# A retention state for the first 256 keys, and a new order for the start of layer 0, in a two-layer hybrid trunk

## The chip, the cores and the metric

The kernel runs on one core of one Trainium2 chip. The metric is the device time of one execution in microseconds (us). The engines are TensorE (PE; its weight loads are listed as PEld), VectorE (DVE), ScalarE (ACT), GpSimd (POOL) and SyncE (SP, whose queue issues most DMAs).

## The reference

Two layers work on 528 positions (16 meta tokens and 512 real ones) of width 1024, all in float32. Each layer: RMSNorm, one input projection, eight heads of forgetting attention (FoX) and four heads of retention, an output projection, then a SwiGLU FFN of width 2816. The last norm drops the meta tokens.

```python
def fox_attention(q, k, v, logf):
    c = cumsum(logf)                              # per head, over positions
    s = q_t.k_s / sqrt(64) + c[t] - c[s]          # s <= t, else -inf
    return softmax(s) @ v
def retention_chunkwise(q, k, v):
    # o_t = sum_{s<=t} gamma_h^(t-s) (q_t.k_s) v_s
    # computed by chunks: inside a chunk directly, older chunks by a state
    state = chunk_dec * state + (k * k_dec)^T v
    ...
def hybrid_layer(h, ...):
    xn = rmsnorm(h, attn_norm_g)
    fq, fk, fv, flog, rq, rk, rv, rg = split(xn @ w_in)
    logf = log_sigmoid(flog + b_fgate)
    fox_out = fox_attention(fq, fk, fv, logf)
    ret = head_groupnorm(retention(rotate(rq), rotate(rk) * 128**-0.5, rv))
    h = h + concat(fox_out, silu(rg) * ret) @ w_out
    hn = rmsnorm(h, ffn_norm_g)
    return h + (silu(hn @ w_gate) * (hn @ w_up)) @ w_down
```

## The kernel before, in words

Activations lie transposed: features on the 128 partitions, the 528 positions along the free axis; `h[0..7]` hold the residual. Every product is made of float32 operands that are split into a rounded high part (`fp32r`) and a low rest, so one product takes three matmuls (high x high, high x low, low x high). The high part is a ScalarE copy, the low part a VectorE subtraction (`split`, lines 150 and 151); for weights it is `convert` (lines 199 and 202, the latter on GpSimd where the job says `pool`).

A projection of 128 output columns is eight steps, one per 128 features, of six matmuls each: three pairs over the column halves of 264 (line 225), or three over 512 columns where only real positions count. Results go to `psd`, two double banks of PSUM; scores and smaller products use `psa`, four banks. The order of TensorE's work is written out by hand: `layer` makes a list of steps, and `merge` puts attention's and retention's steps between the projection's steps at given places. The other engines' order comes from a scheduler that takes instructions by program order and readiness; `tc.high_priority()` moves an instruction forward, and `pin` keeps those that it marks in program order.

**Start of layer 0.** The scaled `x` and the weights are built while the first DMAs land. TensorE then runs the first head pair's queries and keys step by step side by side (`qk`), the forget gates' product (line 389), the norm's column sums (line 298), and goes on with the values and with retention's first projections. The norm's factor `R` (`col_rstd`: Ln, Exp and one Newton step) comes late, so the query and key results wait in `psd` for `R`: `q_done` (line 442) and `k_done` (line 456) scale them straight out of PSUM. `forget_sums` (lines 403 to 412) makes the log-sigmoid of the gates, its running sum `z2`, and the split of it into `f_tiles`. `k_done` puts that, chosen per head by `pick`, into the key tile's other rows ("own rows", line 467). The first FoX scores (line 519) need them. The order was

```python
plan += [squares] + qk[:-2] + [first_parts] + gates + qk[-2:] + stats
        + [queries scaled] + sums + [keys scaled]
plan += v + [ropes]
```

**Retention of a head** (`ret_steps`): `values` transposes and centres the values; `scores` multiplies a key block of 128 by all queries at or after it (line 722), then by the decay table `dec` (line 727), and splits the result into `rsh` and `rsl`; `product` multiplies by the values (line 756). Key blocks start at 0, 128, 256, 384 and 512 (the last has 16 keys). Score steps take the blocks (0), (1) and (2, 3, 4); a block's width is 528, 400, 272, 144 and 16 queries (512 for block 0 in layer 1, which drops the meta queries). The result is copied out of PSUM to `d` by ScalarE (line 764). Ten steps per head are placed by `ret_places` (values, three scores, three products, weighing, norm, gate).

**End.** The last FFN product is made in two column parts, of 272 and 240 positions. For the second the squares of the eight `h` tiles are summed: tiles 0 to 4 on VectorE into `acc`, tiles 5, 6 and 7 separately, and TensorE adds the four parts with a matrix of ones in float32 (line 1164). The root, its Newton step and the output multiplies and DMAs follow.

Of the kernel before, what the change touches and what calls it, by code (L numbers as in the profile page):

```python
# [34 lines left out]
HALF = T // 2  # L35
PSTEP = 416
# [3 lines left out]
def hybrid_kernel(ctx, tc, x_t, w_in, w_fl, w_out, w_gate, w_up, w_down, vecs, b_fg, rope, decay, mask, ident, out_t):  # L40
# [14 lines left out]
    nc.vector.memset(msk[:, 0:T - 128], 0.0)  # L55
# [11 lines left out]
    nc.vector.memset(onec, 1.0)  # L67

# [136 lines left out]
    def dense_steps(src, parts, pool=False, banks=False, ahead=(1, 4), own=None, wait=None):  # L205

        j = len(jobs)
        jobs.append({"src": src, "pool": pool, "own": own})  # L210

        def chunk(k0, k, n, xs, cols, ps, done):
            def go():
                convert(j)
                if k == 0:
                    t = [psum_a() for _ in cols] if banks else psum()
                    ps.append(t)
                    ps.append(t if banks else [t[:, b] for b in range(2)])
                size = jobs[j]["w"][0][0]
                _, hi, lo = jobs[j]["w"][(k0 + k) // size]  # L220
                wk = (k0 + k) % size
                xh, xl = xs(k)
                for i, (w, x) in enumerate(((hi, xh), (hi, xl), (lo, xh))):
                    for b, (c0, c1) in enumerate(cols):
                        nc.tensor.matmul(ps[1][b][:, 0:c1 - c0], w[:, wk, :], x[:, c0:c1],  # L225
                                         start=(k == 0 and i == 0), stop=(k == n - 1 and i == 2))
                if k == n - 1:
                    done(ps[0]) if wait is None else wait.append(lambda: done(ps[0]))
# [62 lines left out]
    def col_rstd(parts, n, cols, rname):  # L291
# [63 lines left out]
    def rstd(st, cols, rname="R"):  # L355

        st["R"] = col_rstd(st["parts"], D, cols, rname)
# [41 lines left out]
    def forget_sums(l, st):  # L399
        z = st["z"]  # L400
        z2 = tt("z2")[0:FH]
        with ExitStack() if l else tc.high_priority():
            nc.vector.scalar_tensor_tensor(z, z, RSC, st["R"][0:FH, :], ALU.mult, ALU.mult)
            nc.scalar.activation(z2, z, AF.Abs, bias=bfg[:, l:l + 1])
            nc.scalar.activation(z2, z2, AF.Exp, scale=-1.0)
            nc.scalar.activation(z2, z2, AF.Ln, bias=onec[0:FH])
        nc.vector.tensor_scalar(z, z, bfg[:, l:l + 1], 0.0, ALU.add, ALU.min)
        nc.vector.tensor_sub(z, z2, z)
        nc.vector.tensor_tensor_scan(z2, z, z, 0.0, ALU.add, ALU.max)
        with ExitStack() if l else tc.high_priority():  # L410
            nc.scalar.copy(f_tiles[0][0:FH], z2)
            nc.vector.tensor_sub(f_tiles[0][32:32 + FH], z2, f_tiles[0][0:FH].bitcast(F32))
# [20 lines left out]
    def fox_dense(l, g, ly, real, st):  # L433
# [5 lines left out]
        def q_done(ps):  # L439
            tq = tt("tq")  # L440
            with tc.high_priority() if first else ExitStack():
                nc.vector.scalar_tensor_tensor(sv(tq, real), pv(ps, real), RSC / 8.0, sv(ly["R"], real), ALU.mult, ALU.mult)  # L442
# [11 lines left out]
        def k_done(ps):  # L454
            tk = tt("tq")
            nc.vector.scalar_tensor_tensor(sv(tk, False), pv(ps, False), RSC, sv(ly["R"], False), ALU.mult, ALU.mult)
            st["k"] = []
            for s in range(2):
# [8 lines left out]
                (nc.gpsimd if g else nc.vector).tensor_scalar(kc[b0:b0 + 32 + FH, :], f_tiles[0].bitcast(F32), pick[:, hd:hd + 1], 0.0, ALU.mult, ALU.add)  # L467
# [156 lines left out]
    def ret_dense(l, hd, ly, real, st, which):  # L624
        QC = REAL if real else FULL

        def rope_done(nm, rl):
            def go(ps):
# [4 lines left out]
                t1 = tt("tq")  # L633
# [5 lines left out]
                st[nm] = (th, tl)  # L639
            return go  # L640
# [7 lines left out]
        def g_done(ps):  # L648
# [10 lines left out]
            nc.vector.tensor_scalar_max(u, x, -80.0)  # L659
# [11 lines left out]
    def ret_steps(l, hd, st, real):  # L671
# [23 lines left out]
        def q_start(j):  # L695
            return max(qlo, KOFF[j] if j < 4 else SEQ)


        def scores(grp):
            if grp[0] == 0:  # L700
                dec = at("dec", F32, (128, T), 1)
                nc.sync.dma_start(dec, decay[hd])
                st["dec"] = dec
# [4 lines left out]
            ps = None  # L708
            reads = []
            for j in grp:  # L710
                q0 = q_start(j)
                d0 = q0 - KOFF[j]
                n = T - q0
                kn = KLEN[j]
                for c0, c1 in (((0, HALF), (HALF, n)) if n > 512 else ((0, n),)):
                    if ps is None or n > 512:
                        ps = psum_a()
                    off = used if len(grp) > 1 else 0
                    sc = ps[0:kn, off:off + c1 - c0]
                    ko = KOFF[j]  # L720
                    for i, (a, b) in enumerate(((kh, qh), (kh, ql), (kl, qh))):
                        nc.tensor.matmul(sc, a[:, ko:ko + kn], b[:, q0 + c0:q0 + c1], start=(i == 0), stop=(i == 2))  # L722
                    reads.append((kn, slice(used + c0, used + c1), sc, slice(d0 + c0, d0 + c1)))
                kept[j] = (used, grp[0])
                used += n
# [14 lines left out]

        def product(grp):
# [4 lines left out]
            po, d = st["po"], st["d"]  # L746
            for j in grp:
                used, g0 = kept[j]
                q0 = q_start(j)
                qa = max(q0, META)  # L750
                sh, sl = kept["t", g0]
                if j == 4:
                    nc.tensor.matmul(po[:, SEQ - META:SEQ], vh[:, 4, :], kept["e"], start=False, stop=True)
                else:
                    for i, (a, b) in enumerate(((vh, sh), (vh, sl), (vl, sh))):
                        nc.tensor.matmul(po[:, qa - META:SEQ], a[:, j, :], b[:, used + qa - q0:used + T - q0],  # L756
                                         start=(j == 0 and i == 0), stop=False)
                if j == 0 and not real:
# [3 lines left out]
                    nc.scalar.copy(d[:, 0:META], pm[:, 0:META])  # L762
                if j == 4:
                    nc.scalar.copy(d[:, META:T], po)
# [55 lines left out]
    def ffn(l, st, real, last):  # L820
# [269 lines left out]
        else:  # L1090
# [34 lines left out]
            def square_b(m):  # L1125
                if m == 0:
                    t = fft("S", F32, (128, 6, w), 2)
                    fin["one"] = [t[:, i, 0:nb] for i in range(3)]
                    fin["acc"], fin["rb"], fin["tb"] = (t[:, i, 0:nb] for i in range(3, 6))
                    d = fin["acc"]  # L1130
                elif m < NK - 3:
                    fin["sq", m] = d = tt("sq")[:, 0:nb]
                else:
                    d = fin["one"][m - NK + 3]
# [111 lines left out]
    def layer(l):  # L1246
# [59 lines left out]
        stats = [lambda: rstd(ly, FULL)]  # L1306
# [5 lines left out]

        sums = [lambda: forget_sums(l, ly)]
# [7 lines left out]
        def ret_places(hd, *places):  # L1321

            f = rs[hd]
            return list(zip(places, (f[0], f[1], f[2], f[4], f[3], f[5], f[6], f[7], f[8], f[9])))
# [29 lines left out]
def _tables():  # L1354
# [4 lines left out]
    decay = np.zeros((RH, 128, T), np.float64)  # L1359
    k = np.arange(128)[:, None]  # L1360
    q = np.arange(T)[None, :]
    for hd in range(RH):
        decay[hd] = np.where(q >= k, np.exp(np.maximum(q - k, 0) * math.log(GAMMA[hd])), 0.0)
    decay = (decay * 128.0 ** -0.5).astype(np.float32)
# [59 lines left out]
```

## Time and profile before

| | us |
|---|---|
| median of 3 runs | 1268.74 (1267.4 to 1270.0) |
| profiled execution, device time | 1268.53 |
| its span, first to last instruction | 1266.7 |

| engine | busy us | share of the span |
|---|---|---|
| PE | 1251.2 | 99% |
| PEld | 1194.1 | 94% |
| DVE | 991.9 | 78% |
| ACT | 704.8 | 56% |
| POOL | 273.3 | 22% |

Matmuls are pipelined: a matmul's listed duration is longer than the distance to the next one's start, and the distance is what counts. In the timeline a row has the start, the duration, the engine and line, the operation, output and inputs, and in brackets how long the engine idled before it and what ended that. "x2" means that two instructions were merged into the row. PEclk is the granted share of TensorE's full clock. A line of the profile can be that of a helper.

### The profile page before, as it was taken

How to read it: one execution, taken by the hardware profiler on the slowest of the kernel's cores; microseconds unless marked ns; L12 is line 12 of the kernel's file. 1: busy time of each engine (PE TensorE's matmuls, PEld its weight loads, DVE VectorE, ACT ScalarE, POOL GpSimd, SP SyncE). 2: the span in 40 equal slices, each digit the busy share in tenths (PEclk: the TensorE clock that was granted, in tenths of full speed). 3: DMA queues.
4: the chain of work that ended last, by engine and by line, in shares of the span. 5: the costliest groups of instructions: out<-in, count | busy, mean ns of one | idle time of the engine just before them, and what ended most of it. 6: DMA issues, size and time to landing. Idle time of an engine off the chain costs nothing.

```text
span 1266.7 us, 23526 instructions
## 1 busy us (share of the span) xinstructions
PE 1251.2 (99%) x9225; PEld 1194.1 (94%) x9225; DVE 991.9 (78%) x1804; ACT 704.8 (56%) x1301; POOL 273.3 (22%) x539
## 2 busy tenths in 40 slices
PE   9999999999999999999999999999999999999997
PEld 8899999999999999999999989998789999999996
DVE  8887756779988888887786877567899888888867
ACT  6766655676444444444466766557764444444445
POOL 3455546420000000000126556554100000000000
PEclk9999999999999999999999999999999999999999
DMA  6122222223333333332322122222223333333321
GB/s 218 50 76 75 76 77 72 72 67 118 104 97 100 100 101 100 101 101 84 101 77 84 60 86 74 70 90 67 100 94 123 100 101 101 100 101 101 100 84 67
DMA packets 43342, 116.19 MB, mean 92 GB/s; under 512 B 5088, under 2 KB 12000, under 8 KB 43232
## 3 DMA queue, kind: packets, MB, share of 16 engines
q1 hardware_dynamic: 42800, 114.41, 28.1%
q8 instruction: 72, 1.18, 0.4%
q14 instruction: 38, 0.31, 0.1%
q10 hardware_dynamic: 432, 0.29, 0.1%
HBM read 112.58 MB, written 2.10 MB: 91 GB/s over the span
## 4 chain that ended last, share of the span: by engine, by line
PE 93%; ACT 3%; DVE 3%; issue 1%; DMA 0%; ACTq 0%; DVEq 0%
PE psd L225 30%; PE psa L907 18%; PE psd L1042 14%; PE psd L907 13%; PE psa L225 5%; PE psa L1042 4%; PE psa L429 2%; PE psa L519 2%; PE psa L589 1%; PE psa L756 1%; PE psa L722 1%; ACT whi L199 1%; PE psa L298 0%; ACT xh L327 0%; DMA raw<-w_in 0%
## 5 line engine op out<-in xcount | busy, mean ns | idle before, releaser
L202 POOL TENSOR_TENSOR wlo<-raw,whi 128x128 fp32r<-128x128 f32 x504 | 258.2, 548 | 260.1 <-ACT whi L199 259.7
L225 PE MATMUL psd<-xh,whi 128*128 128x264 f32 (+1 forms) x792 | 195.5, 314 | 0.2 <-DVE tq L442 0.2
L225 PE MATMUL psd<-xl,whi 128*128 128x264 f32 (+1 forms) x792 | 186.7, 303 | 0.6 <-DVE xl L328 0.6
L225 PE MATMUL psd<-xh,wlo 128*128 128x264 f32 (+1 forms) x792 | 187.0, 304 | 0.0
L225 PEld LDWEIGHTS psd<-xh,whi 128*128 128x128 f32 x792 | 128.6, 189 | 5.0 <-issue 0.6
L225 PEld LDWEIGHTS psd<-xh,wlo 128*128 128x128 f32 x792 | 127.2, 188 | 6.2 <-DVE wlo L202 0.4
L225 PEld LDWEIGHTS psd<-xl,whi 128*128 128x128 f32 x792 | 127.8, 189 | 5.4 <-DVE xl L328 1.4
L199 ACT CAST whi<-raw 128x512 fp32r<-128x512 f32 (+1 forms) x168 | 97.9, 613 | 41.5 <-PE psd L225 28.4
L895 ACT CAST whi<-raw 128x1024 fp32r<-128x1024 f32 (+2 forms) x62 | 54.9, 885 | 51.3 <-PE psd L907 39.8
L895 ACT CAST fwhi<-raw 128x1024 fp32r<-128x1024 f32 (+2 forms) x62 | 55.6, 897 | 47.5 <-PE psd L907 40.0
L122 POOL MEMSET kc<- 64x528 f32 x2 | 1.1, 533 | 345.4 <-PE psa L907 345.4
L896 DVE TENSOR_TENSOR wlo<-raw,whi 128x1024 fp32r<-128x1024 f32 (+2 forms) x62 | 62.9, 1014 | 12.7 <-ACT whi L895 12.6
L896 DVE TENSOR_TENSOR fwlo<-raw,fwhi 128x1024 fp32r<-128x1024 f32 (+2 forms) x62 | 64.0, 1032 | 11.1 <-ACT fwhi L895 10.9
L907 PE MATMUL psa<-th,whi 128*128 128x264 f32 (+1 forms) x232 | 65.4, 282 | 0.0
L907 PE MATMUL psa<-th,wlo 128*128 128x264 f32 (+1 forms) x232 | 65.4, 282 | 0.0
L907 PE MATMUL psa<-tl,whi 128*128 128x264 f32 (+1 forms) x232 | 65.3, 282 | 0.0
L907 PE MATMUL psa<-th,fwhi 128*128 128x264 f32 (+1 forms) x224 | 63.4, 283 | 0.0
L907 PE MATMUL psa<-tl,fwhi 128*128 128x264 f32 (+1 forms) x224 | 63.3, 283 | 0.0
L907 PE MATMUL psa<-th,fwlo 128*128 128x264 f32 (+1 forms) x224 | 63.2, 282 | 0.0
L536 ACT ACTIVATE pr<-pr,nmax 128x144 f32<-128x144 f32 (+1 forms) x64 | 36.8, 576 | 45.4 <-DVE nmax L523 26.1
L895 ACT CAST fwhi<-S 128x1024 fp32r<-128x1024 f32 x20 | 21.0, 1049 | 68.6 <-PE psa L907 66.5
L973 ACT COPY e<-psa 128x264 f32<-128x264 f32 (+1 forms) x114 | 42.8, 376 | 28.4 <-PE psa L907 24.1
(365 smaller groups left out, 4041.2 us busy)
## 6 DMA issues: line engine op xcount, KB each, us to landing
raw<-w_in SPq DMA_DIRECT2D x54, 512.0 KB, 3.5
raw<-w_gate SPq DMA_DIRECT2D x44, 512.0 KB, 3.9
fraw<-w_up SPq DMA_DIRECT2D x38, 512.0 KB, 3.5
raw<-w_down SPq DMA_DIRECT2D x64, 256.0 KB, 2.9
raw<-w_out SPq DMA_DIRECT2D x16, 512.0 KB, 3.4
raw<-w_down SPq DMA_DIRECT2D x32, 192.0 KB, 2.5
raw<-w_up SPq DMA_DIRECT2D x6, 512.0 KB, 3.5
h<-x_t SPq DMA_DIRECT2D x8, 264.0 KB, 4.5
```

The lines of the kernel that those rows point to most:

```text
L199: pin(nc.scalar.copy(hi, job["raw"][:, c0:c1]), pinned)
L202: pin(sub(lo[:, c:c + step], job["raw"][:, c0 + c:c0 + c + step], hi[:, c:c + step].bitcast(F32)), pinned)
L225: nc.tensor.matmul(ps[1][b][:, 0:c1 - c0], w[:, wk, :], x[:, c0:c1], start=(k == 0 and i == 0), stop=(k == n - 1 and i == 2))
L429: nc.tensor.transpose(ps[:, 128 * j:128 * j + 128], src[:, o:o + 128], idt)
L519: nc.tensor.matmul(sc[0:nq, 0:c1 - c0], qq[:, q0:q0 + nq], kk[:, c0:c1], start=(i == 0), stop=(i == 1))
L536: nc.scalar.activation(pr, pr, AF.Exp, bias=nmax[0:nq], scale=-1.0, accum_out=rsum)
L589: nc.tensor.matmul(po[:, c0:SEQ], v[:, j, :], pp[:, j, META + c0:T], start=(j == 0 and i == 0), stop=(j == 4))
L895: nc.scalar.copy(hi, src)
L896: nc.vector.tensor_sub(lo, src, hi.bitcast(F32))
L907: nc.tensor.matmul(bank()[:, 0:b.shape[-1]], a[:, o + k, :], b, start=(fresh and k == 0 and i == 0), stop=(k == n - 1 and i == 2), skip_gr ...
L973: nc.scalar.copy(self.t["e"][:, i], self.t["x"][:, 0:w])
L1042: nc.tensor.matmul(v[:, 0:c1 - c0], a[:, s * n + k, :], b[:, c0:c1], start=(k == 0 and i == 0), stop=(k == n - 1 and i == 2))
```

## The change

Three groups of edits. **Retention:** keys 0 to 255 no longer meet the queries from 256 on directly. Their keys are transposed and weighted by decay (`keys`), multiplied with their values into a 128 x 128 state (`memory`), and the second `product` multiplies that state with the queries from 256 on. The score steps are (0, 1), now up to query 256 only, and (2, 3, 4), whose decay table no longer depends on the query; the query's decay is applied when the result leaves PSUM, on VectorE. The step list is again ten long: values, scores (0, 1), keys, memory, scores (2, 3, 4), product (0, 1), product (2, 3, 4), weigh, norm, gate, in the places of before. The table grows from 528 to 962 columns, and the float32 keys are kept in a tile of their own, `rkf`.

**Layer 0's start:** the first queries and keys are copied aside, unscaled, by ScalarE (`aside`); the next weights' cast is pinned behind the copies; the gates' chain comes before the scaling of queries and keys; one subtraction of the chain is folded into the scan; the chain's rest gets high priority; the norm's Ln and Exp are pinned; the second head's own rows go to ScalarE.

**Small orders:** the mask's memset goes to GpSimd; the gate's lower bound is made by another VectorE instruction; at the end tile 5's square is added on VectorE, and three parts go to TensorE instead of four.

```diff
+CUT = 256
+DOFF = (0, 0, CUT, T, 2 * T - CUT - 128)
+DEC = DOFF[4] + META + T - CUT + 2
...
-    nc.vector.memset(msk[:, 0:T - 128], 0.0)
...
+    nc.gpsimd.memset(msk[:, 0:T - 128], 0.0)
...
-                nc.scalar.activation(r[:, c0:c1], v, AF.Ln, bias=epsc, scale=1.0 / n)
-            nc.scalar.activation(r[:, c_all], r[:, c_all], AF.Exp, scale=-0.5)
+                pin(nc.scalar.activation(r[:, c0:c1], v, AF.Ln, bias=epsc, scale=1.0 / n), pinned)
+            pin(nc.scalar.activation(r[:, c_all], r[:, c_all], AF.Exp, scale=-0.5), pinned)
...
-        nc.vector.tensor_scalar(z, z, bfg[:, l:l + 1], 0.0, ALU.add, ALU.min)
-        nc.vector.tensor_sub(z, z2, z)
-        nc.vector.tensor_tensor_scan(z2, z, z, 0.0, ALU.add, ALU.max)
-        with ExitStack() if l else tc.high_priority():
+            nc.vector.tensor_scalar(z, z, bfg[:, l:l + 1], 0.0, ALU.add, ALU.min)
+            nc.vector.tensor_tensor_scan(z2, z2, z, 0.0, ALU.add, ALU.subtract)
             nc.scalar.copy(f_tiles[0][0:FH], z2)
...
-            tk = tt("tq")
-            nc.vector.scalar_tensor_tensor(sv(tk, False), pv(ps, False), RSC, sv(ly["R"], False), ALU.mult, ALU.mult)
+            tk = ps if first else tt("tq")
+            nc.vector.scalar_tensor_tensor(sv(tk, False), sv(ps, False) if first else pv(ps, False), RSC, sv(ly["R"], False), ALU.mult, ALU.mult)
...
-                (nc.gpsimd if g else nc.vector).tensor_scalar(kc[b0:b0 + 32 + FH, :], f_tiles[0].bitcast(F32), pick[:, hd:hd + 1], 0.0, ALU.mult, ALU.add)
+                own, of = kc[b0:b0 + 32 + FH, :], f_tiles[0].bitcast(F32)
+                if g:
+                    nc.gpsimd.tensor_scalar(own, of, pick[:, hd:hd + 1], 0.0, ALU.mult, ALU.add)
+                elif s:
+                    nc.scalar.activation(own, of, AF.Copy, scale=pick[:, hd:hd + 1])
+                else:
+                    with tc.high_priority():
+                        nc.vector.tensor_scalar(own, of, pick[:, hd:hd + 1], 0.0, ALU.mult, ALU.add)
...
-            nc.vector.tensor_scalar_max(u, x, -80.0)
+            nc.vector.scalar_tensor_tensor(u, x, -80.0, x, ALU.max, ALU.max)
...
-        def q_start(j):
-            return max(qlo, KOFF[j] if j < 4 else SEQ)
+        def q_range(j):
+            return max(qlo, KOFF[j]), (CUT if KOFF[j] < CUT else T)
...
+        def keys():
+            (_, n, p3), = transpose_into(st["rkf"], KOFF[0:2])
+            th, tl = (at(f"rt{i}", shape=(128, 2, 128)) for i in "hl")
+            for j in range(n):
+                g = st["dec"][:, DEC - 2 + j:DEC - 1 + j]
+                nc.scalar.activation(th[:, j], p3[:, j], AF.Copy, scale=g)
+                nc.vector.scalar_tensor_tensor(tl[:, j], p3[:, j], g, th[:, j].bitcast(F32), ALU.mult, ALU.subtract)
+            st["kt"] = th, tl
+
+        def memory():
+            (th, tl), (vh, vl) = st["kt"], st["rv"]
+            ps = psum_a()[:, 0:128]
+            for j in range(2):
+                for i, (a, b) in enumerate(((th, vh), (th, vl), (tl, vh))):
+                    nc.tensor.matmul(ps, a[:, j, :], b[:, j, :], start=(j == 0 and i == 0), stop=(j == 1 and i == 2))
+            mh, ml = (at(f"rm{i}", shape=(128, 128)) for i in "hl")
+            split(mh, ml, ps)
+            st["memory"] = mh, ml
...
+            if grp[0]:
+                (mh, ml), (qh, ql) = st["memory"], st["rq"]
+                for i, (a, b) in enumerate(((mh, qh), (mh, ql), (ml, qh))):
+                    nc.tensor.matmul(po[:, CUT - META:SEQ], a, b[:, CUT:T], start=(i == 0), stop=False)
...
+                if j == 1:
+                    nc.scalar.copy(d[:, META:CUT], po[:, 0:CUT - META])
                 if j == 4:
-                    nc.scalar.copy(d[:, META:T], po)
+                    with tc.high_priority():
+                        nc.vector.tensor_mul(d[:, CUT:T], po[:, CUT - META:SEQ], st["dec"][:, DEC - 2 - T + CUT:DEC - 2])
...
-        G = ((0,), (1,), (2, 3, 4))
-        return [values] + [lambda g=g: scores(g) for g in G] + [lambda g=g: product(g) for g in G] + [weigh, head_norm, gate]
+        G = ((0, 1), (2, 3, 4))
+        return [values, lambda: scores(G[0]), keys, memory, lambda: scores(G[1]),
+                lambda: product(G[0]), lambda: product(G[1]), weigh, head_norm, gate]
...
+                sum_b(5)
                 v = psum_a()[:, 0:nb]
-                sums(v, [fin["one"][0], fin["acc"]] + fin["one"][1:])
+                sums(v, [fin["one"][0], fin["acc"], fin["one"][1]])
...
+        def aside():
+            for i, (ps, done) in enumerate(ly["wait"]):
+                t = tt("tq")
+                pin(nc.scalar.copy(sv(t, False), pv(ps, False)))
+                ly["wait"][i] = t, done
+            convert(4, NK, True)
...
-            plan += [lambda: squares(ly, FULL, True, False)] + qk[:-2] + [first_parts] + gates + qk[-2:] + stats + [lambda: ly["wait"].pop(0)()] + sums + [lambda: ly["wait"].pop(0)()]
+            plan += [lambda: squares(ly, FULL, True, False)] + qk[:-2] + [first_parts] + gates + qk[-2:] + stats + [aside] + sums + [scaled] * 2
...
-            m0, r0, places = (((7 if l else 10.5, 31 if l else 32.5), (34, 40.5), (13, 33.5, 35.5, 37.5, 39, 40.5, 43, 44, 47.5, 48)),
+            m0, r0, places = (((7 if l else 11, 31 if l else 32.5), (34, 40.5), (13, 33.5, 35.5, 37.5, 39, 40.5, 43, 44, 47.5, 48)),
```

More of the change, by code (lines that the diff above doesn't have):

```diff
@@ L227, in go @@
                 if k == n - 1:
-                    done(ps[0]) if wait is None else wait.append(lambda: done(ps[0]))
+                    done(ps[0]) if wait is None else wait.append((ps[0], done))
                 for half, at_step in enumerate(ahead):
@@ L289, in col_parts, with col_rstd @@
         return sh, sl
-    def col_rstd(parts, n, cols, rname):
+    def col_rstd(parts, n, cols, rname, pinned=False):
         c_all = slice(cols[0][0], cols[-1][1])
@@ L353, in squares, with rstd @@
             st["parts"] = col_parts(acc, cols)
-    def rstd(st, cols, rname="R"):
-        st["R"] = col_rstd(st["parts"], D, cols, rname)
+    def rstd(st, cols, rname="R", pinned=False):
+        st["R"] = col_rstd(st["parts"], D, cols, rname, pinned)
     def mix_tile(i):
@@ L707, in scores @@
             used = 0
-            ps = None
+            ps = psum_a()
             reads = []
             for j in grp:
-                q0 = q_start(j)
-                d0 = q0 - KOFF[j]
-                n = T - q0
+                q0, q1 = q_range(j)
+                d0 = DOFF[j] + q0 - KOFF[j]
+                n = q1 - q0
                 kn = KLEN[j]
[L715 to L724, printed above, removed]
+                sc = ps[0:kn, used:used + n]
+                ko = KOFF[j]
+                for i, (a, b) in enumerate(((kh, qh), (kh, ql), (kl, qh))):
+                    nc.tensor.matmul(sc, a[:, ko:ko + kn], b[:, q0:q1], start=(i == 0), stop=(i == 2))
+                reads.append((kn, slice(used, used + n), sc, slice(d0, d0 + n)))
+                kept[j] = used
                 used += n
@@ L1311, in first_parts, with scaled @@
             convert(3, NK, True)
+        def aside():
[4 more added lines that the diff above has]
+            convert(4, NK, True)
+        def scaled():
+            t, done = ly["wait"].pop(0)
+            done(t)
         sums = [lambda: forget_sums(l, ly)]
```

44 lines of the change are left out of this document (25 added, 19 removed).

## The prediction

> **What bounds the kernel now.** I read the page's head and busy times first, then TensorE's waits, then the stretches round the one long wait, then the chain through that place, and last the start times of retention's matmuls. A row of a stretch holds its limits and length, the busy time of PE, PEld, DVE, ACT and POOL with their counts, the granted clock, the DMA share and GB/s.
>
> ```profile
> span 1266.7 us, 23526 instructions
> PE 1251.2 (99%) x9225; PEld 1194.1 (94%) x9225; DVE 991.9 (78%) x1804; ACT 704.8 (56%) x1301; POOL 273.3 (22%) x539
> PE psa L519 <- DVE kc L467: 3.1, 1, 3.1
> PE psa L756 <- DVE rsl L151: 0.7, 2, 0.4
> 37.50:41.00 3.50, 0.43 (x6) 0.42 (x6) 3.37 (x6) 1.22 (x4) 3.06 (x6) 1.00 0.01 2
> 41.00:46.00 5.00, 5.00 (x32) 5.00 (x31) 2.66 (x13) 1.97 (x8) 1.21 (x3) 0.66 0.30 105
> 46.00:60.00 14.00, 13.95 (x115) 13.73 (x114) 11.46 (x39) 11.18 (x30) 6.58 (x12) 1.00 0.11 39
> ```
>
> TensorE (PE) is busy 99% of the span, so only two things shorten the kernel: work taken off TensorE, or its few waits. The one long wait is in layer 0: 3.1 us, for the gates' own rows that L467 writes into the key tile `kc`. While it lasts VectorE (DVE) is busy 3.37 of 3.50 us. A second cost stands right behind: from 41 to 46 us the granted clock is 0.66, though it is 1.00 in the stretches on both sides. Five us at 0.66 lose 5.0 x 0.34 = 1.7 us. The Trainium skill, "TensorE: Matmul & The Clock Gate" (Part 1), says that an idle window of some 3.4 us sets the array to half clock; this row, after 3.1 us of idling, agrees roughly.
>
> A row of TensorE's timeline gives one small wait ahead of it, for the first query bank:
>
> ```profile
> 29.34 0.48 PE L225 MATMUL psd<-xh,whi 128*128 128x264 f32 x2 [0.25 <-DVE tq L442]
> ```
>
> All that layer 0's head can give back is thus 3.1 + 0.25 + 1.7 = 5.0 us.
>
> **Part 1, the gates' chain.** Pieces of the chain that ended last (start, us, what), then the chain's operations with shortest, median and longest duration:
>
> ```profile
> 1.66 4.51 DMA raw<-w_in
> 24.54 0.51 ACT whi L199
> 28.49 0.72 DVE tq L442
> 37.45 0.71 DVE sr L1258
> 39.80 0.67 DVE kc L467
> L403 DVE SCALAR_TENSOR_TENSOR z<-z,R x2: 696/840/983, 29.1 to 659.0; 8x528 f32<-8x528 f32 x2
> L404 ACT ACTIVATE z<-z,bfg x2: 734/736/737, 30.3 to 659.7; 8x528 f32<-8x528 f32 x2
> L405 ACT ACTIVATE z<-z x2: 645/646/647, 31.7 to 660.5; 8x528 f32<-8x528 f32 x2
> L406 ACT ACTIVATE z<-z,onec x2: 735/736/737, 33.0 to 661.2; 8x528 f32<-8x528 f32 x2
> L408 DVE TENSOR_TENSOR z<-z,z x2: 685/692/699, 34.2 to 661.9; 8x528 f32<-8x528 f32 x2
> L409 DVE TENSOR_TENSOR_SCAN z<-z x2: 1239/1272/1305, 35.4 to 663.2; 8x528 f32<-8x528 f32 x2
> L411 ACT CAST fs<-z x2: 632/632/633, 36.7 to 664.6; 8x528 fp32r<-8x528 f32 x2
> L412 DVE TENSOR_TENSOR fs<-z,fs x2: 704/772/840, 38.2 to 665.3; 8x528 fp32r<-8x528 f32 x2
> ```
>
> Before, the queries' scaling starts at 28.49, and the first own rows are done at 39.80 + 0.67 = 40.47: 12.0 us. The chain's own operations in this order are 0.72 (queries first), 0.98, 0.74, 0.65, 0.74, 0.69, 1.24, 0.63, 0.84, 0.67 = 7.9 us. The other 4.1 us are work that got in between; `sr`, the scaling of the rope table, is such a piece.
>
> After: the Ln and Exp of the norm are pinned, so the weight cast of 0.51 us no longer sits between them, and R is there at about 27.9. The gates come before the queries (-0.72), and the subtraction L408 goes, folded into the scan (-0.69). The bare chain is then 6.5 us and would end at 34.4. The filling will not vanish: the same query, key, value and rope operations wait for the same R. I take half of it, 2.1 us, since the minimum and the scan are now of high priority too and the second head's own rows go to ScalarE (ACT): own rows at 36.5. TensorE began to wait at 40.5 - 3.1 = 37.4 and comes 0.25 earlier, at 37.15, so that wait goes. With all of the filling it is 38.5, a wait of 1.4 us. What is late next are the value transposes some 2 us on: the values of fox and of retention's first head are scaled on VectorE after all this. I put 0.8 us on these leftovers: 5.0 - 0.8 = **4.2 us gained**, bounds 1.6 (the clock drops as before and 1.7 us of waits remain) and 5.0.
>
> The copies aside: two copies out of PSUM on ScalarE, and two casts of the next weight pinned behind them. The nearest row is the 512-wide copy below, 0.58 us; two make 1.2 us, two casts of weights, like the one on the chain, 1.0 to 1.2. They fall into ScalarE's pause before the queries:
>
> ```profile
> L764 ACT COPY d<-psa x8: 580/583/587, 80.7 to 884.8; 128x512 f32<-128x512 f32 x8
> 29.23 0.63 ACT L449 CAST qo<-tq 64x528 fp32r<-64x528 f32 x1 [3.64 <-DVE tq L442]
> 22.70 9.24 POOL L202 TENSOR_TENSOR wlo<-raw,whi 128x128 fp32r<-128x128 f32 x16 [20.73 <-ACT whi L199]
> ```
>
> 2.4 us in a pause of 3.64: hidden, and the bank is free before TensorE asks for it (the 0.25). If the pause were full, Abs of the gates would wait behind them, at most 2.4 us. ScalarE's version of the own rows (no row before; 0.6 to 0.8 like its neighbours above) belongs to the second head and is hidden unless ScalarE falls behind. The mask's memset goes to GpSimd (POOL), whose next work is at 22.70 after 20.73 idle: zero there; on VectorE it frees one memset at the very start, where the chain waits for the first weights' DMA (4.51 us from 1.66): zero.
>
> **Part 2, retention.** Start-to-start distances of one head in layer 0:
>
> ```profile
> 66.01 0.28 PE L722 MATMUL psa<-rqh,rkh 128*128 128x264 f32 x1
> 66.13 0.28 PE L722 MATMUL psa<-rql,rkh 128*128 128x264 f32 x1
> 68.41 0.35 PE L722 MATMUL psa<-rqh,rkh 128*128 128x400 f32 x1
> 68.59 0.34 PE L722 MATMUL psa<-rql,rkh 128*128 128x400 f32 x1
> 70.99 0.40 PE L756 MATMUL psa<-rsl,rvh 128*128 128x512 f32 x1
> 71.22 0.39 PE L756 MATMUL psa<-rsh,rvl 128*128 128x512 f32 x1
> 73.33 0.23 PE L722 MATMUL psa<-rqh,rkh 128*128 128x144 f32 x1
> 73.39 0.27 PE L722 MATMUL psa<-rql,rkh 128*128 128x144 f32 x1
> 73.50 0.28 PE L722 MATMUL psa<-rqh,rkl 128*128 128x144 f32 x1
> 79.17 0.29 PE L756 MATMUL psa<-rsh,rvh 128*128 128x272 f32 x1
> 79.30 0.28 PE L756 MATMUL psa<-rsl,rvh 128*128 128x272 f32 x1
> ```
>
> So 264 columns cost 0.12 us, 272 0.13, 400 0.18, 512 0.23; but 144 columns cost 0.06 for the first of a run and 0.11 for those behind. Short matmuls do not get cheaper in proportion.
>
> Removed per head: scores of the first key block 6 x 0.12 = 0.72 (layer 1: 3 x 0.23 = 0.69), of the second 3 x 0.18 = 0.54; products 3 x 0.23 = 0.69 and 3 x 0.18 = 0.54. Sum 2.5 us. Added: scores at 256 columns 3 x 0.12 = 0.36 and at 128 0.06 + 2 x 0.11 = 0.28; two transposes 0.2; the state, six matmuls of 128, 0.06 + 5 x 0.11 = 0.61; products at 240 columns 0.36 and 128 0.28; the state times the queries 3 x 0.13 = 0.39. Sum 2.5 us. The columns fall by a fifth, the time by nothing: **0.0 us** over 8 heads. Bounds: all twelve 128-column matmuls at 0.06 give -0.5 per head, -4 us; all at 0.11 +0.15 per head, +1.2. I keep the middle, as rows of both kinds stand in one run.
>
> The Trainium skill has a rule against this part ("TensorE: Matmul & The Clock Gate", Part 2, LDWEIGHTS): loading a stationary operand of 128 columns takes 128/1.2 = 107 ns, however narrow the moving side. The 0.11 here agrees. By the rule alone the six matmuls of the state cost 0.64.
>
> New waits: for head 0 the transposed keys must be split on ScalarE and VectorE (two operations each) within two steps of the merge before the state is built; for head 3 the state must be split before the second product. Both replace waits like the 0.7 us at L756 quoted first. I take +0.5 over both layers for the new and -0.5 for the old: zero, with +3 as the far bound if each head waits 0.4.
>
> Vector work barely moves: the multiplications by decay lose columns, the state adds a split and a scaled eviction. The larger decay table's next load waits for the last product instead of the scores, and on SyncE's (SP) queue weight loads stand behind it:
>
> ```profile
> 75.12 0.33 SPq L702 DMA_DIRECT2D dec<-decay  x1
> 81.90 30.51 SPq L166 DMA_DIRECT2D raw<-w_in  x5
> ```
>
> The last product's eviction was at 80.7 (first L764 above), so this load moves from 75 to about 81.5, just ahead of the weight load that was issued at 81.90 anyway: under 0.5 us on a transfer nobody waits for. Zero. The changed maximum in the gate is a slightly longer VectorE operation for two heads a layer: zero under VectorE's 11.46 of 14.00.
>
> **Part 3, the end.**
>
> ```profile
> 1256.94 1.89 PE L1164 MATMUL psa<-S,ones 128*128 128x240 f32 x8 [0.22 <-ACT S L1135]
> 1257.21 1.99 DVE L1142 TENSOR_TENSOR th<-th,e 128x544 f32<-128x544 f32 x3
> 1259.37 0.41 DVE L1156 TENSOR_TENSOR S<-S 128x240 f32<-128x240 f32 x1 [0.17 <-ACT S L1152]
> ```
>
> Eight matmuls of 1.89 / 8 = 0.24 us become six, but the first then waits for a square that came 0.5 us later; at best 0.1 is won. The added sum (0.4) pushes the three VectorE output multiplies behind it from an end of 1259.20 to 1259.6, and the root's refinement, at 1259.37 before, queues behind them, with some overlap: +0.1, bounds -0.1 and +0.3.
>
> **Sum.** -4.2 + 0.0 + 0.1 = -4.1 us. The profiled execution took 1268.53 us (span 1266.7 and 1.8 around it), 0.2 below the median of 1268.74. 1268.5 - 4.1 = 1264.4 us.
>
> **The rivals.**
> A, the forecast, 1262.5 to 1266.2: the long wait goes, the clock stays at 1.00, retention is even. 0.62.
> B, the head still waits: the filling stays, or the earlier TensorE runs into VectorE at the transposes (11.46 of 14.00 us busy from 46 to 60 speaks for it, the 2.34 us idle from 41 to 46 against), and perhaps the clock drops again. Gain 1.6: 1266.9. 0.18.
> C, retention does win: runs of 128 columns go at 0.06 to 0.09 and its waits go too, 2 to 4 us more: 1261. 0.12.
> D, slower: the state's chain (transpose, two splits, six matmuls, split) becomes a wait in each of the 8 heads. It eats the gain at 4.1 / 8 = 0.5 us per head; 1.0 us per head, the time of one and a half of the 0.7-us vector operations above in a queue, gives 1268.5 - 4.1 + 8 = 1272.4. Against it: most heads have four steps or more between these parts. 0.08.
>
> A measurement of this kernel tells 0.2%, 2.5 us, from no change. Faster by that is A, C and nothing of B: 0.74; within it B and a little of D: 0.19; slower: 0.07. The range takes in B and most of C: 1260.5 to 1268.0.
>
> **What would show it.** Right: no wait of TensorE at L467's own rows, PEclk 1.00 from 41 to 46, the first fox scores near 37 us, retention's matmuls with as much time as before though fewer columns, six matmuls at the end. Wrong: a TensorE wait over 1 us before 50 us, waits for the state's or the keys' splits, 128-column matmuls well away from 0.11.

## The result: slower by 1.2%

| | before | after |
|---|---|---|
| median | 1269.09 us (1267.4 to 1270.0, 4 runs) | 1285.74 us (1284.54 to 1285.94, 4 runs) |
| span of the profiled execution | 1266.7 us | 1284.1 us |

The ratio is 1.0122, with a 95% interval of 1.0109 to 1.0136. The forecast was 1264.4 us, in a range of 1260.5 to 1268.0; it was wrong in sign. The head of the page after, then TensorE's waits (what it waited for, us in total, times, longest):

```profile
span 1284.1 us, 23724 instructions
PE 1258.2 (98%) x9299; PEld 1198.9 (93%) x9299; DVE 993.8 (77%) x1820; ACT 706.7 (55%) x1321; POOL 275.2 (21%) x540
```

```profile
PE psa L776 <- ACT d L793: 6.1, 6, 1.9
PE psa L761 <- DVE rsl L154: 2.6, 1, 2.6
...
PE psa L728 <- DVE rkl L154: 1.4, 1, 1.4
PE psa L761 <- ACT rth L752: 0.9, 1, 0.9
PE psa L1197 <- ACT S L1168: 0.9, 1, 0.9
PE psa L527 <- DVE kc L475: 0.8, 1, 0.8
```

TensorE is busy 7.0 us longer (1258.2 against 1251.2), and the span is 17.4 us longer; the other 10.4 us are idle time. Of the old 3.1 us for the gates' own rows (`kc`) 0.8 are left; the prediction had none left there. At the top stands a wait that the prediction does not have at all: six times L776, the product of the state with the queries, waits for ScalarE's copy L793 of `d`, the output of the *first* product.

The stretches that the prediction showed, and two new ones (limits and length, busy us of PE, PEld, DVE, ACT and POOL, granted clock, DMA share, GB/s):

```profile
37.50:41.00 3.50, 3.00 (x27) 3.03 (x28) 2.71 (x8) 2.09 (x9) 2.71 (x7) 1.00 0.02 6
41.00:46.00 5.00, 4.42 (x35) 4.00 (x34) 4.77 (x16) 3.65 (x12) 1.25 (x4) 1.00 0.32 105
...
72.22:75.63 3.41, 3.41 (x17) 3.32 (x17) 0.63 (x4) 0.76 (x2) 0.00 (x0) 0.50 0.00 0
778.78:782.19 3.41, 3.41 (x18) 3.41 (x17) 2.03 (x4) 1.25 (x2) 0.00 (x0) 0.50 0.82 266
```

From 37.5 to 41 TensorE is busy 3.00 us instead of 0.43, and from 41 to 46 the clock stays at 1.00. But the half clock has moved: there are two stretches of 3.41 us at 0.50, one behind the first state (72.22) and one behind the longest wait for the copy (778.78). TensorE is busy all through both, so each costs half its length, 1.7 us.

Now the timeline of the first head's product (start, us, engine, line; the bracket is idle time and what ended it):

```profile
80.30 0.27 PE L785 MATMUL psa<-rsh,rvl 128*128 128x128 f32 x1
...
83.32 0.39 PE L776 MATMUL psa<-rqh,rmh 128*128 128x272 f32 x1 [1.25 <-ACT d L793]
...
82.38 0.63 ACT L153 CAST mxh<-mixt 128x528 fp32r<-128x528 f32 x1 [0.57 <-DVE mixt L607]
82.92 0.35 ACT L793 COPY d<-psa 128x240 f32<-128x240 f32 x1
```

The first product is finished at about 80.5 (some projection work follows), but its 240 columns are copied only at 82.92, since in ScalarE's queue another cast stands ahead of the copy, and that cast itself waits 0.57 us for VectorE. L776 starts within 0.1 us of the copy's end. It writes columns 240 to 511 of `po`, the copy reads columns 0 to 239 of the same bank, and the program makes the one wait for the other.

And the timeline round the first state:

```profile
62.77 3.37 POOL L205 TENSOR_TENSOR wlo<-raw,whi 128x128 fp32r<-128x128 f32 x8
62.99 3.72 DVE L669 SCALAR_TENSOR_TENSOR ge<-sg 128x528 f32<-128x528 f32 x1
...
65.90 0.38 PE L430 MATMUL psa<-idt,rkf 128*128 128x128 f32 x2
70.90 0.33 PE L761 MATMUL psa<-rvh,rth 128*128 128x128 f32 x1 [2.59 <-DVE rsl L154]
71.55 0.33 PE L761 MATMUL psa<-rvh,rtl 128*128 128x128 f32 x1 [0.21 <-DVE rtl L753]
```

The transposed keys (L430) leave TensorE at about 66.2, the state's matmuls start at 70.90. In between, one VectorE instruction lasts 3.72 us, beside eight subtractions of GpSimd: it is L669, the gate's lower bound, whose median is 0.80 us.

### The profile page after: what moved, and what is told of

It reads as the page before. It is cut to its first block, busy times and chain, and to the rows that moved or that the text cites. A ratio compares the mean times of both kernels' runs of the same rounds, so it can differ in the third digit from the quotient of the medians.

```text
span 1284.1 us, 23724 instructions
## 1 busy us (share of the span) xinstructions
PE 1258.2 (98%) x9299; PEld 1198.9 (93%) x9299; DVE 993.8 (77%) x1820; ACT 706.7 (55%) x1321; POOL 275.2 (21%) x540
## 4 chain that ended last, share of the span: by engine, by line
PE 86%; ACT 4%; DVE 4%; issue 1%; DMA 0%; POOL 0%; DVEq 0%; ACTq 0%
PE psd L228 26%; PE psa L940 18%; PE psd L1075 14%; PE psd L940 13%; PE psa L228 5%; PE psa L1075 4%; PE psa L430 2%; PE psa L527 1%; PE psa L597 1%; ACT whi L202 1%; PE psa L728 1%; PE psa L785 1%; PE psa L776 0%; PE psa L301 0%; ACT mxh L153 0%
## 5 line engine op out<-in xcount | busy, mean ns | idle before, releaser
L929 DVE TENSOR_TENSOR fwlo<-raw,fwhi 128x1024 fp32r<-128x1024 f32 (+2 forms) x62 | 64.0, 1032 | 10.1 <-ACT fwhi L928 10.0
```

What stands on the lines that cost most here:

```text
L929: nc.vector.tensor_sub(lo, src, hi.bitcast(F32))
```

## The experiments

Each difference is taken to the kernel before on the same chip, whose medians were 1270.54 (first four runs), 1270.57 (next four) and 1270.56 us (last three); for the kernel after it is +16.65 us.

| run | median us | to before, us | ratio, 95% interval |
|---|---|---|---|
| after, late copy of `d` | 1280.06 | +9.5 | 1.0061 to 1.0094 |
| after, old maximum | 1284.58 | +14.0 | 1.0098 to 1.0132 |
| before, new start of layer 0 only | 1266.22 | -4.3 | 0.9955 to 0.9981 |
| before, new retention only | 1289.01 | +18.5 | 1.0132 to 1.0162 |
| late copy, first state later | 1276.03 | +5.5 | 1.0028 to 1.0058 |
| late copy, no lower bound | 1276.28 | +5.7 | 1.0030 to 1.0058 |
| all waits mended | 1272.03 | +1.5 | 1.0002 to 1.0021 |
| late copy, no state | 1260.51 | -10.1 | 0.9906 to 0.9936 |
| after, two banks | 1279.45 | +8.9 | 1.0055 to 1.0085 |
| mended, own rows on ScalarE | 1270.90 | +0.3 | 0.9992 to 1.0011 |
| new start, nothing aside | 1267.04 | -3.5 | 0.9958 to 0.9981 |

**1. The copy of `d` later.**

```diff
-                if j == 1:
+                if j == 4:
                     nc.scalar.copy(d[:, META:CUT], po[:, 0:CUT - META])
-                if j == 4:
                     with tc.high_priority():
```

> The changed kernel with one move: ScalarE copies queries 16 to 255 of a head's result out of PSUM after the last product, not between the two products. Theory 'bank': the state's product waits for that copy since both use one PSUM bank; the changed kernel shows 6.1 us of such waits in 6 heads and a clock drop behind one of them (half clock for 3.4 us, 1.7 us lost). Expected 1278.0 us (1276.5 to 1280), no TensorE wait for the copy. Rival 'short matmuls' (runs of 128 columns, bound by weight loads, are what costs): no change, 1285 us. Rival 'moved': the wait turns into one for the split of the state or for the scores' low part, 1282 us or more.

Measured: 1280.06 us, 7.1 less than after by the differences to before. The time lies at the upper end of what was expected (1280). TensorE no longer waits for the copy; what is left at L776 is the state's own split:

```profile
PE psa L761 <- DVE rsl L154: 2.6, 1, 2.6
...
PE psa L776 <- DVE rml L154: 0.7, 2, 0.3
PE psa L776 <- ACT rmh L153: 0.4, 1, 0.4
```

The first state now meets 6.8 us at half clock (70.2 to 77.0) instead of 3.4, so the copy's own price is somewhat above 7.1.

**2. The gate's lower bound as before.**

```diff
-            nc.vector.scalar_tensor_tensor(u, x, -80.0, x, ALU.max, ALU.max)
+            nc.vector.tensor_scalar_max(u, x, -80.0)
```

> The changed kernel with the gate's lower bound made by the old one-input VectorE instruction. Theory 'maximum': in the changed kernel one of the four two-input instructions lasted 3.7 us while GpSimd split a weight, and the scores and keys of retention's first head stood behind it; without it the 2.6 us wait of the state's matmuls at 68 us shrinks to that of layer 1 (0.9 us) and the clock stays up: 1282.0 us (1281 to 1283.5). Rival 'keys too close': the state of the first head is built two steps after its keys are transposed, so the wait stays without the long instruction: 1285 us.

Measured: 1284.58 us; the interval overlaps that of after. The theory that the new form of the instruction is to blame falls; the old form stands there as long:

```profile
63.77 3.44 DVE L669 TENSOR_SCALAR ge<-sg 128x528 f32<-128x528 f32 x1
```

**3 and 4. Each half of the change alone.** Run 3 has the whole start of layer 0 (the gates' chain first, own rows, copies aside) with the old retention, end and maximum; run 4 the reverse.

```diff
 (run 3, on the kernel before; the gates' chain and own rows as in the change)
-            plan += ... + stats + [lambda: ly["wait"].pop(0)()] + sums + [lambda: ly["wait"].pop(0)()]
+            plan += ... + stats + [aside] + sums + [scaled] * 2
 (run 4, on the kernel before; scores, keys, memory, product and decay as in the change)
-        G = ((0,), (1,), (2, 3, 4))
+        G = ((0, 1), (2, 3, 4))
```

> The kernel before with the new start of layer 0 alone (copies aside, gates first, pins, ScalarE's own rows). Theory 'start gains': TensorE's wait of 3.1 us falls under 1 us and the clock stays at 1.00: 4 us faster, 1265.0 us (1264 to 1266). Rival 'given back': TensorE comes earlier but VectorE is late at the transposes and the time is 1267 to 1269. Rival 'start costs': slower than 1270.

> The kernel before with the retention state alone. Theory 'retention costs': all that was lost, and the gain of the start that hid a part, is here, less what the long maximum cost: 1284 to 1288 us, with the waits for the copy (some 6 us) and for the keys. Rival 'together': the two parts only cost when TensorE comes earlier; then retention alone stays within 1268 to 1275.

Measured: -4.3 and +18.5 us (1266.22 and 1289.01 us, 0.2 and 1.0 above what was expected). The start gains what was forecast (4.2), and the clock in that kernel does not drop before the end. The stretches of run 3:

```profile
37.50:41.00 3.50, 3.06 (x27) 3.09 (x28) 2.65 (x8) 2.10 (x9) 2.77 (x7) 1.00 0.01 2
41.00:46.00 5.00, 4.40 (x34) 3.98 (x33) 4.83 (x16) 3.64 (x13) 1.24 (x4) 1.00 0.32 105
```

So retention makes the loss. It costs 18.5 us beside the old start, whose clock drops near 40 us as ever; beside the new one retention, the end and the small orders together cost 16.65 + 4.3 = 21.0. The 2.5 us between these two were not settled.

**5. The first head's state later** (on top of run 1).

```diff
-  (34, 40.5), (13, 33.5, 35.5, 37.5, 39, 40.5, 43, 44, 47.5, 48)),
+  (34, 40.5), (13, 33.5, 35.5, 39.5, 39, 41.5, 43, 44, 47.5, 48)),
```

> The kernel after with the late copy of d (1280.06 us), and the first head's state built two steps of the merge later (its first product one step later). Theory 'spacing': the transposed keys and the state stand too close in the first head of each layer; the waits of 2.6 us in layer 0 and 0.9 us in layer 1 go, and with them most of the 6.8 us at half clock behind the first (3.4 us lost): 1274 to 1277 us. Rival 'VectorE is late anyway': the operation of 3.7 us on VectorE delays all that follows, and the wait only moves to the next step: 1279 to 1280.5 us.

Measured: 1276.03 us, 4.1 less by the differences to before. The waits at L761 are gone in both layers and the clock does not drop. But the VectorE instruction still lasts 3.72 us, and part of the wait moves to the next scores, here 1.4 us:

```profile
PE psa L728 <- DVE ptl L154: 1.4, 1, 1.4
```

So both theories hold a part: with more room the wait at the state goes, but VectorE is as late as before.

**6. No lower bound** (on top of run 1).

```diff
-            nc.vector.scalar_tensor_tensor(u, x, -80.0, x, ALU.max, ALU.max)
-            nc.scalar.activation(u, u, AF.Exp, scale=-1.0)
+            nc.scalar.activation(u, x, AF.Exp, scale=-1.0)
```

> The kernel after with the late copy of d, and without the lower bound of the gate on VectorE (the bound at -80 is left out: Exp reads the gate itself). Theory 'lock-out': the 3.1 us that VectorE stood still beside GpSimd's eight subtractions are the wait; the wait of 2.6 us at the first state falls under 0.5 and the half clock behind it is shorter: 1275 to 1277.5 us against 1280.06. Rival 'spacing': the state's wait stays above 1.5 us: 1279 to 1280.5. Third: the next VectorE operation is shut out instead, and nothing changes.

Measured: 1276.28 us, 3.8 less, with a wait of 1.4 us at the first state instead of 2.6 and 3.41 us at half clock behind it instead of 6.83. The time is the first theory's, but the wait did not fall under 0.5, and the trace shows the third as well: the next VectorE instruction, on one column, is shut out in its turn:

```profile
62.19 3.38 POOL L205 TENSOR_TENSOR wlo<-raw,whi 128x128 fp32r<-128x128 f32 x8
62.52 3.07 DVE L536 TENSOR_TENSOR nmax<-nmax 128x1 f32<-128x1 f32 x1
```

Its median in this run is 0.16 us. VectorE comes free at 65.6 instead of 66.3, with the bound's work left out.

**7. All known waits mended**: runs 5 and 6 together, the last head's scores one step later and its state 1.5 steps earlier, the old order of the last sums.

```diff
-  ret_places(3, 52, 45.5, 47.5, 57.5, 55.5, 58.5, 60, 64.1, 63, 64.2))
+  ret_places(3, 52, 46.5, 48.5, 56, 55.5, 58.5, 60, 64.1, 63, 64.2))
```

> The kernel after with the late copy of d, the first head's state two steps later, the lower bound of the gate left out, the last head's scores one step later and its state 1.5 steps earlier, and the old order of the last sums. Theory 'waits and matmuls': all waits that retention added are gone, what stays is its TensorE time, 5 to 6 us above the old retention's: 1266.2 + 5.5 = 1270.5 to 1273 us, still slower than the kernel before by 0.1 to 0.3%. Rival 'waits alone' (the prediction's zero for the matmuls): 1265.5 to 1268. Rival 'scattered': new waits appear elsewhere: 1275 or more.

Measured: 1272.03 us, in the first theory's range, and still 0.1% above the kernel before. The longest wait that retention has left is 1.1 us.

**8. No state at all** (on top of run 1): the steps `keys` and `memory` and the three matmuls of the state with the queries are taken out, so the queries from 256 on lack the keys before 256.

```diff
-                (mh, ml), (qh, ql) = st["memory"], st["rq"]
-                for i, (a, b) in enumerate(((mh, qh), (mh, ql), (ml, qh))):
-                    nc.tensor.matmul(po[:, CUT - META:SEQ], a, b[:, CUT:T], start=(i == 0), stop=False)
...
-        return [values, lambda: scores(G[0]), keys, memory, lambda: scores(G[1]),
+        return [values, lambda: scores(G[0]), lambda: None, lambda: None, lambda: scores(G[1]),
```

> The kernel after with the late copy of d, without the state of the keys 0 to 255: no transposed keys, no state, no product of the state with the queries (the queries from 256 on then miss these keys). What the shorter scores and products save by themselves, against 1266.22 us with the old retention and the new head: by the prediction's prices 8 x (2.5 - 1.28) = 9.8 us, 1256.5; by the sums of TensorE's time in the traces 34.8 - 27.4 = 7.4 us, 1258.8. The difference to 1280.06 is the whole price of the state's chain: 12.9 us of matmuls and some 8 us of waits and clock. If the waits and the clock did not belong to the chain, 1264 or more.

Measured: 1260.51 us. The shorter scores and products save 5.7 us against run 3's kernel (which has the old end and small orders), less than both prices in the expectation (9.8 and 7.4). The price itself was right: if the time of each of retention's matmuls is counted from its start to TensorE's next start, or to its own end where a gap follows, they take 34.4 us in run 3's trace and 24.6 in this one. The heads of the two pages, run 3 first, show that TensorE's busy time falls by only 7.1 us of these 9.8, and that its idle time (span less busy) rises from 14.0 to 16.2:

```profile
span 1263.6 us, 23526 instructions
PE 1249.6 (99%) x9225; PEld 1192.2 (94%) x9225; DVE 990.7 (78%) x1800; ACT 706.5 (56%) x1305; POOL 272.9 (22%) x539
```

```profile
span 1258.7 us, 23489 instructions
PE 1242.5 (99%) x9211; PEld 1184.8 (94%) x9211; DVE 985.9 (78%) x1796; ACT 699.9 (56%) x1297; POOL 278.2 (22%) x540
```

So other matmuls and waits take back 4 to 5 us; which, was not settled. The state's chain costs 1280.06 - 1260.51 = 19.6 us.

**9. Two banks** (on the kernel after).

```diff
             if grp[0]:
+                po = psum_a()
                 (mh, ml), (qh, ql) = st["memory"], st["rq"]
```

> The kernel after with one edit: the second product of retention (state times queries and the later blocks) goes to a PSUM bank of its own, and the copy of d stays where it is, ahead of the second product. Theory 'bank': the wait for the copy comes from both products sharing a bank, not from ScalarE being busy as such; with two banks the copy no longer holds TensorE: near the kernel with the late copy (1280.06 us), 1278 to 1281. Rival 'banks run short': the additional bank in a rotation that other products use is claimed too early, and the wait only changes its name: 1283 to 1286.

Measured: 1279.45 us. The copy stays where it was, ScalarE is as busy (706.7 us in both), and the wait for it is gone: sharing `po` was the cause, not ScalarE being busy. A stretch of 3.41 us at half clock stands at 711.03 here, behind the wait for the state in layer 1, instead of at 778.78.

**10. Another moment for GpSimd** (run 7 with the bound back on VectorE).

```diff
-                if g:
-                    nc.gpsimd.tensor_scalar(own, of, pick[:, hd:hd + 1], 0.0, ALU.mult, ALU.add)
-                elif s:
+                if g or s:
                     nc.scalar.activation(own, of, AF.Copy, scale=pick[:, hd:hd + 1])
```

> The kernel with all waits mended (1272.03 us), with the gate's lower bound back on VectorE and the later heads' own rows moved from GpSimd to ScalarE, so that GpSimd's eight subtractions start about 0.6 us earlier against VectorE's work. Theory 'chance of the moment': VectorE is shut out for 3.0 to 3.7 us only when its instruction starts right after GpSimd's run does; with other moments no VectorE instruction there is longer than 1.3 us, and 1 to 2 us are gained: 1269.5 to 1271.5. Rival 'whenever they meet': an instruction of VectorE is again shut out for about 3 us: 1271.5 to 1273.5.

Measured: 1270.90 us. The same VectorE instruction now takes 0.71 us, 0.74 us into GpSimd's run, and TensorE is busy without a gap from 60 to 72:

```profile
61.58 3.86 POOL L205 TENSOR_TENSOR wlo<-raw,whi 128x128 fp32r<-128x128 f32 x8 [4.36 <-ACT whi L202]
62.32 0.71 DVE L667 SCALAR_TENSOR_TENSOR ge<-sg 128x528 f32<-128x528 f32 x1
```

```profile
60.00:72.00 12.00, 12.00 (x103) 11.91 (x103) 9.23 (x27) 9.63 (x24) 5.24 (x11) 1.00 0.13 48
```

Instructions can meet without being shut out, against the rival; GpSimd's eight subtractions took 3.86 us here instead of 3.37. The time is 1.1 us under run 7's by the differences to before, but the two intervals overlap. The new retention is now within 0.1% of the kernel before, with a start that is worth 4.3 us by itself.

**11. The start without the copies aside** (on run 3): `aside` only makes the weights' cast, and VectorE scales the queries and keys out of PSUM as before.

> The kernel before with the new start of layer 0 only (1266.22 us), without the copies of the first queries and keys out of PSUM (VectorE scales them out of PSUM as before; the gates' chain still comes first). The prediction counted the copies at 0.25 us. Theory 'small': 1266.2 to 1267. Rival 'the copies are needed': with the gates' chain ahead, the queries hold their bank longer than before, TensorE waits for it 1 to 3 us and the clock drops again: 1268 to 1271.

Measured: 1267.04 us, 0.8 above run 3 by the differences to before; the intervals overlap. The wait for the query bank is back, at 0.6 us:

```profile
PE psd L225 <- DVE tq L440: 0.6, 1, 0.6
```

The copies matter little, as forecast; the rest of the new start carries the gain.

Of all versions that compute the whole result the best is the kernel before with the new start of layer 0 alone: 1266.22 us, ratio 0.9968 (0.9955 to 0.9981), faster than both kernels.

## Why the prediction was wrong, step by step

**The start of layer 0: right in size, in part by luck.** Forecast 4.2 us, measured 4.3 (by the interval 2.4 to 5.7). In the changed kernel R was ready at 27.5 (27.9 forecast), TensorE arrived at 37.2 (37.15), and the first own rows were done at 37.9, not 36.5. From R to the own rows it took 10.3 us, of which the chain's own operations are 6.3: about 4 us of filling stayed, all of it and not half, and the scaling of `sr` still stands right ahead. That left the wait of 0.8 us. The forecast had 0.8 us of leftovers too, but at the transposes; that the two sizes agree is luck. The clock's 1.7 us came back in full.

**The step that failed: "new waits: zero".** The waits were set at +0.5 for the new and -0.5 for the old, with +3 as the far bound. The change lost 21.0 us outside layer 0's start, and the runs divide them so, by their differences to before:

| step | us |
|---|---|
| wait for the copy out of the shared bank (after to run 1) | 7.1 |
| state too close behind the keys in the first head (run 1 to 5) | 4.1 |
| rest of VectorE's lateness, last head, end (run 5 to 7) | 4.0 |
| VectorE still shut out beside GpSimd (run 7 to 10; within the intervals) | 1.1 |
| what is left against the new start alone (run 10 to 3) | 4.7 |
| sum: retention, the end and the small orders | 21.0 |

So at least the first two rows, 11.2 us, are waits and the clock behind them, against a far bound of 3. The largest was not among the rivals. The working followed what retention *waits for* (keys, state) and priced the copy only as the date of the table's next load, 80.7. It did not ask what the copy, moved into the middle of a product, holds up: a bank that TensorE goes on writing. The diff shows `po` shared by both products and a copy between them. The Trainium skill has the rule ("PSUM — Partial Sum Buffer", "PSUM bank collisions raise a hardware error"): two engines must be kept apart by bank, not by address. This program keeps to that rule: the matmuls on columns 240 to 511 waited up to 1.9 us for a reader of columns 0 to 239, and with a second bank they did not. The second bank is also a second tile of the program, so no run here shows whether the wait goes by the bank or by the tile.

Rival D named the state's chain as a wait, at 1.0 us per head in all eight. It was 2.6 us in one head and 0.9 in another, and the half clock behind the first added 1.7 us (3.4 in run 1). Its chance, 0.08, was far too low, and its argument against ("most heads have four steps or more") looked at most heads where the first of each layer decides.

**The matmuls: prices and sum right.** Six matmuls of the state run as forecast (0.06 for the first, 0.11 for the others; 0.62 in all), here from run 10:

```profile
125.90 0.23 PE L759 MATMUL psa<-rvh,rth 128*128 128x128 f32 x1
125.96 0.27 PE L759 MATMUL psa<-rvl,rth 128*128 128x128 f32 x1
126.07 0.28 PE L759 MATMUL psa<-rvh,rtl 128*128 128x128 f32 x1
126.19 0.27 PE L759 MATMUL psa<-rvh,rth 128*128 128x128 f32 x1
126.30 0.28 PE L759 MATMUL psa<-rvl,rth 128*128 128x128 f32 x1
126.41 0.28 PE L759 MATMUL psa<-rvh,rtl 128*128 128x128 f32 x1
126.52 0.22 PE L587 MATMUL psa<-pth,vv 128*128 128x16 f32 x1
```

Counted as in run 8, retention's matmuls take 34.4 us in run 3's trace and 34.6 in run 10's: 0.2 more, where zero was forecast. So a state that saves a fifth of the columns saves nothing even without waits. (With the gaps between these matmuls it is 34.8 and 36.4.) The 4.7 us between the two kernels are thus not the price of retention's matmuls. The head of run 10's page, to be held against that of run 3 above, has 4.4 us more of busy time and 0.9 us more of idle time:

```profile
span 1268.9 us, 23700 instructions
PE 1254.0 (99%) x9301; PEld 1195.9 (94%) x9301; DVE 989.5 (78%) x1819; ACT 715.9 (56%) x1333; POOL 267.0 (21%) x528
```

Some 4 us therefore lie in the time of the other matmuls, spread over the stretches in which heads are worked on. Why these take longer stays open.

**Small terms.** The decay table's load was issued at 85.25 instead of 75, 4 us later than forecast, and no instruction waited for it. The end was forecast at +0.1 and took 0.26 us longer from the last FFN matmul on: six matmuls of 0.25 instead of eight, but behind a wait of 0.89 instead of 0.22 us:

```profile
1274.77 1.48 PE L1197 MATMUL psa<-S,ones 128*128 128x240 f32 x6 [0.89 <-ACT S L1168]
```

The maximum at zero was right for its form (run 2) and wrong in its place, where VectorE was shut out.

## What to carry to other kernels

Where a result's copy moves between two groups of matmuls, ask first whether the second group writes the same PSUM bank: here TensorE waited for that copy, and for all that stood ahead of it in the copying engine's queue; a second bank, or a copy after the last write, took the wait away here. Price a longer dependency chain at the place where its steps stand closest (the first head), not by the average head, and add the clock: in the changed kernel the wait of 1.9 us cost 3.6 with the half clock behind it, and that of 2.6 us cost 4.3. Time saved on single matmuls does not all reach the kernel (5.7 us here, where retention's matmuls became 9.8 us shorter), and a state has to be paid from that.

## What the runs showed of the hardware

**VectorE shut out by GpSimd.** In ten of the thirteen profiles one VectorE instruction at this place lasted 3.0 to 3.7 us, until GpSimd's run of eight subtractions was over or nearly so, whatever the instruction (528 columns, or a single one); before, run 3 and run 10 show none. The Trainium skill ("SBUF — State Buffer", "SBUF: two separate sides") says that the later one is blocked for the other's whole instruction. The trace agrees that it is a block and not a slowdown, but the block lasted seven or eight GpSimd instructions of about 0.42 us, not one. It is no mark of the new retention: run 11, with the old one, has it too (3.03 us). What decides whether VectorE gets in between two of them is open.

**Half clock after less idling than thought.** Between 40 and 1240 us each stretch at 0.50 lasts 3.41 us (or two of them), and the starts within one profile lie whole multiples of it apart (72.22 and 778.78: 207 x 3.413). The idle time of TensorE in the 3.41 us ahead of a stretch was 1.8 to 2.8 us in eleven of fourteen cases, and on this grid no full clock followed more than 1.4 us of idling in the 3.41 us before. The Trainium skill ("TensorE: Matmul & The Clock Gate", Part 1) has the free-running window of 3413 ns, and the trace agrees; but half a window of idling was enough here, not a whole one (2.35 us in the kernel before, where the prediction took the 3.1 us to agree). Three stretches came after only 1.0 to 1.1 us and remain unexplained; as much idling in the changed kernel (1.03 us ahead of 140.48) left the clock at full.
